# Hybrid conv and gated-delta-rule block: writing a head's 1/rms to DRAM as columns, straight from its SBUF tile

## The chip, the cores and the metric

The kernel runs on one core of one Trainium2 chip. The metric is the device time of one execution in microseconds (us). The kernel before was timed in three runs: median 1574.67 us, from 1572.23 to 1576.7.

## What is computed

Two layers work on 256 context tokens and 1024 main tokens of width 1024. A layer normalises and modulates its input, multiplies it by `w_in`, and splits the product into a convolution branch (31 taps, layer norm, gate) and four heads of a gated delta rule in both directions of time. Both branches are multiplied by `w_out` and added to the input. The part that matters here ends each head:

```
o = (o_f + flip(o_b)).transpose(0, 2, 1, 3)
zg = jax.nn.silu(z.reshape(bsz, t, DN_HEADS, DN_HEAD_DIM))
o = rms_norm(o, norm_w) * zg       # y * rsqrt(mean(y*y) + EPS) * norm_w
```

So each token of each head needs one number, 1/rms over its 128 channels, by which the head's output is multiplied.

## The kernel before, in words

All 1280 tokens lie on the free axis, in ten blocks of 128; channels lie on the 128 partitions. Layer 0 works on ten blocks, layer 1 on the eight blocks of the main tokens where the result is concerned (`xb0` = 2).

The work of a layer is cut into steps, and a string per layer in `PLAN` names their order: `K`, `Q`, `V`, `Z` are projections of a head (L376, TensorE; `Z` stores the gate to `gdr`), `A` the short convolution and the norms, `B` the inverse of a triangular matrix (its elimination runs on VectorE, L706 and L708, ends in the transposes L712 and L713, and TensorE takes it up at L729), `D` the decay rows and attention blocks, `R` the recurrence over the blocks, `N` the norm of the head's output, `C` and `T` the convolution's projections and its taps (L538, VectorE), `G` the convolution's gates, `L` its layer norm, `W` the first loads of `w_out`. The output projection (L1022) follows. `LEAD` lifts some steps' priority by a number of instructions, and `ADA_AT` says after which weight groups a slice of the modulation weights is loaded. From these priorities the order of every engine's instructions is fixed when the program is built; on the chip each engine and each DMA queue works its own list strictly in order and waits on semaphores.

Step `N` is `head_norm` (L883 on). It adds the two directions (L894, VectorE), squares (L895, ScalarE), sums over the channels with a matmul against ones, so that token sums stand as columns (L897, through L169), and loads the gate `sz` (L898, the queue of GpSimd). VectorE makes 1/rms in `st[:, 1]`, a tile of 128 partitions (tokens of a block) by ten or eight columns (blocks), with eleven small operations and three rounds of Newton's method (L899, L140 to L145). For heads 0 to 2 the columns have to become one row that lies on all partitions: TensorE turns them into ten rows of 128 (L903), ScalarE copies these out of PSUM (L905) and issues their store to a row of the DRAM tile `rdr` (L907), and GpSimd's queue reads the row back onto all partitions into `rb` (L908). `rb` is the buffer `qg[1]`, `sz` the buffer `qg[0]`, and the next head's step `D` loads its rows into the same two buffers (L665). VectorE then multiplies by the gate (L911) and by `rb` (L921), and GpSimd's queue stores the result to `ydr` (L922). Head 3 spreads its columns with matmuls instead (L918) and is not touched. There are six of these turns, three in each layer.

Of the kernel before, what the change touches and what calls it, by code (L numbers as in the profile page):

```python
# [8 lines left out]
F32 = mybir.dt.float32  # L9
# [4 lines left out]
AF = mybir.ActivationFunctionType  # L14
# [10 lines left out]
NB = T // 128  # L25
# [17 lines left out]
for _name, _w in (("nw", DEPTH * KT), ("bada", DEPTH * 24), ("cw", DEPTH * 4 * CW), ("cb", DEPTH * 4),  # L43
# [7 lines left out]


PLAN = (
# [4 lines left out]
)  # L58

ADA_AT = ((0, 2, 4, 6, 7, 8, 9, 10, 11, 12, 13, 14, 15, 16, 17, 18, 19, 20, 21, 22, 23, 24, 26, 27), (0, 3, 10, 14, 15, 16, 19, 22))


LEAD = {'O': 300, 'A': 700, 'B': 450, 'D': 1000, 'L': 1200, 'M': 0, 'N': 500, 'R': 1000, 'W': 2550}


def pos(b):
    return b * 128 + (4 if b >= 2 else 0)
# [3 lines left out]
def mixer_kernel(ctx: ExitStack, tc: tile.TileContext, xs, cst_d, wada, win, wab, gp_d, wout, fnw, out):  # L73
    nc = tc.nc
    dve, act, pool, pe = nc.vector, nc.scalar, nc.gpsimd, nc.tensor
# [6 lines left out]
    def bank(tag, bufs, shape=(128, 512)):  # L82
        return ps.tile(list(shape), F32, tag=tag, name=tag, bufs=bufs)

    def misc(shape=(128, 512)):
        return bank("pb", 2, shape)
# [4 lines left out]
    def cols(shape):  # L91
        return bank("pa", 1, shape)
# [8 lines left out]
    ident = cp.tile([128, 128], F32, name="ident")  # L101
# [35 lines left out]
    def rsqrt_small(y, x, t):  # L137

        yi = y.bitcast(I32)
        dve.tensor_scalar(out=yi, in0=x.bitcast(I32), scalar1=1, scalar2=None, op0=ALU.logical_shift_right)  # L140
        dve.tensor_scalar(out=yi, in0=yi, scalar1=-1, scalar2=0x5F3759DF, op0=MUL, op1=ADD)
        for _ in range(3):
            dve.tensor_tensor(out=t, in0=y, in1=y, op=MUL)
            dve.scalar_tensor_tensor(out=t, in0=t, scalar=-0.5, in1=x, op0=MUL, op1=MUL)
            dve.scalar_tensor_tensor(out=y, in0=t, scalar=1.5, in1=y, op0=ADD, op1=MUL)  # L145
# [21 lines left out]
    def colsum(o, w, i, start=True, stop=True):  # L167

        pe.matmul(o[:, i:i + 128], lhsT=w, rhs=ones, start=start, stop=stop)  # L169
# [3 lines left out]
    def ada_load(l, g):  # L173
        w = wp.tile([128, KT, 128], F32, tag="wst", name="wst", bufs=3)
        nc.sync.dma_start(w, wada[l, g])
        return l, g, w
# [154 lines left out]
    def later(n, f, *a):  # L331
        for _ in range(n):
            yield 1
        f(*a)
# [9 lines left out]
    def load_w(l, g, invh):  # L344
# [6 lines left out]
        if nxt_ < len(GORDER) and GORDER[nxt_][0] == l:  # L351
            prefetch(GORDER[nxt_])
            active.append(later(0, split, GORDER[nxt_]))
        if (nxt_ - 1) % (len(GORDER) // DEPTH) in ADA_AT[l]:
            held.append(ada_load(*ADA[l].pop(0)))
# [42 lines left out]
    for l in range(DEPTH):  # L398
        last = l == DEPTH - 1
        segs = XSEGS if last else SEGS  # L400
        xb0 = 2 if last else 0
        lay = ExitStack()
        hd = lay.enter_context(tc.tile_pool(name=f"hd{l}", bufs=1, side="right"))
# [479 lines left out]
        def head_norm(h, kq, ob, qg, zsc):  # L883


            t_ = qg[0].rearrange("p a b -> p (a b)")
            rb = qg[1].rearrange("p a b -> p (a b)")

            sz = t_ if h < HEADS - 1 else hd.tile([128, T], F32, tag="tmp", name="sz", bufs=4)
            pss = cols((128, NB + 127))  # L890
            st = hd.tile([128, 3, NB], F32, tag="ost", name="ost", bufs=1)
            for t0, n, v_ in segs:
                o = kq[:, 1, pos(t0 // 128):pos(t0 // 128) + n]
                dve.tensor_tensor(out=o, in0=o, in1=ob.rearrange("p a b -> p (a b)")[:, t0:t0 + n], op=ADD)  # L894
                act.activation(t_[:, t0:t0 + n], o, AF.Square)  # L895
                for b in range(t0 // 128, (t0 + n) // 128):
                    colsum(pss, t_[:, b * 128:(b + 1) * 128], b)  # L897
            nc.gpsimd.dma_start(sz[:, segs[0][0]:], gdr[l][4 + h][:, segs[0][0]:])  # L898
            dve.tensor_scalar(out=st[:, 0, xb0:], in0=pss[:, xb0:NB], scalar1=1.0 / 128, scalar2=EPS, op0=MUL, op1=ADD)  # L899
            rsqrt_small(st[:, 1, xb0:], st[:, 0, xb0:], st[:, 2, xb0:])  # L900
            if h < HEADS - 1:
                pr = cols((NB, 128))
                pe.transpose(pr[0:NB - xb0, :], st[:, 1, xb0:], ident)  # L903
                ro = hd.tile([4 * NB, 128], F32, tag="rt", name="ro", bufs=1)
                act.activation(ro[0:NB - xb0, :], pr[0:NB - xb0, :], AF.Copy)  # L905
                dr = rdr[l][16 + h:17 + h, xb0 * 128:]
                nc.scalar.dma_start(dr.rearrange("r (b t) -> (r b) t", t=128), ro[0:NB - xb0, :])  # L907
                nc.gpsimd.dma_start(rb[:, xb0 * 128:], dr.partition_broadcast(128))  # L908
            for t0, n, v_ in segs:
                o = kq[:, 1, pos(t0 // 128):pos(t0 // 128) + n]  # L910
                dve.scalar_tensor_tensor(out=o, in0=o, scalar=zsc[:, v_:v_ + 1], in1=sz[:, t0:t0 + n], op0=MUL, op1=MUL)  # L911
                if h < HEADS - 1:
                    src = rb[:, t0:t0 + n]
                else:
                    src = misc()[:, 0:n]
                    for j in range(n // 128):
                        b = t0 // 128 + j
                        pe.matmul(src[:, j * 128:(j + 1) * 128], lhsT=st[:, 1, b:b + 1].to_broadcast([128, 128]),  # L918
                                  rhs=ident, start=True, stop=True)
                if h < HEADS - 1:  # L920
                    dve.tensor_tensor(out=o, in0=o, in1=src, op=MUL)  # L921
                    nc.gpsimd.dma_start(ydr[l][4 + h][:, t0:t0 + n], o)  # L922
                else:
                    dve.tensor_tensor(out=olast[0][:, t0:t0 + n], in0=o, in1=src, op=MUL)
# [4 lines left out]
        def emit(step):  # L929
            k, i = step[0], int(step[1:] or 0)  # L930
            if k in "KQV":
                head_proj(i, "KQV".index(k))
            elif k == "A":
                with after("elim"):
                    prep[i] = head_a(i)
            elif k == "B":
                inv[i] = head_b1(i, prep[i][0], prep[i][2])
            elif k == "D":
                b2[i] = head_b2(i, *prep[i])
            elif k == "R":  # L940
                head_rec(i, prep[i][0], prep[i][2], inv[i], *b2[i])
            elif k == "N":
                head_norm(i, prep[i][0], b2[i][2][:, 1], b2[i][3], zs[i])
            elif k == "Z":
                zs[i] = head_z(i)
            elif k == "C":
                us[i] = conv_proj(i)
            elif k == "T":
                with after("elim"):
                    conv_taps(i // 3, i % 3)  # L950
            elif k == "G":
                conv_gate(i)
            elif k == "W":
                early_wout()
            elif k == "L":
                conv_norm(i)

        for step in PLAN[l].split():
            with tc.high_priority(LEAD[step[0]]) if step[0] in LEAD else nullcontext():
                emit(step)  # L960
# [10 lines left out]
        with tc.tile_pool(name=f"op{l}", bufs=1, side="right", reuse_waits="tile") as op:  # L971
# [20 lines left out]
            def out_tile(tt, tag):  # L992
                i = (tt - xb0) % 2
                y = place(f"y{i}", 896).rearrange("p (k t) -> p k t", t=128)
                yh, yl = (place(f"{t_}{i}", DM, F32R).rearrange("p (k t) -> p k t", t=128) for t_ in ("yh", "yl"))
                return tt, y, yh, yl, [bank(tag, 2) for _ in range(2)]
# [58 lines left out]

            with tc.high_priority(LEAD["O"]):
                two = [out_tile(xb0, "pj"), out_tile(xb0 + 1, "rc")]
# [33 lines left out]
            for tt in range(xb0 + 2, NB):  # L1091
                t = out_tile(tt, "pj")
# [73 lines left out]
```

## Time and profile before

| | |
|---|---|
| median of three runs | 1574.67 us |
| the profiled execution | 1572.46 us, of which the span is 1570.8 us |
| TensorE (PE) | busy 1457.3 us, 93% of the span |
| VectorE (DVE) | busy 1253.7 us, 80% |
| ScalarE (ACT) | busy 896.0 us, 57% |
| GpSimd (POOL) | busy 145.1 us, 9% |
| mean granted TensorE clock | 0.976 |

A share of busy time is a mean over stages that have different limits, so what a change is worth has to be read from the stretch in which it stands. A time in brackets behind an instruction is how long its engine sat idle before it, and the name after the arrow is what ended that wait.

### The profile page before, as it was taken

How to read it: one execution, taken by the hardware profiler on the slowest of the kernel's cores; microseconds unless marked ns; L12 is line 12 of the kernel's file. 1: busy time of each engine (PE TensorE's matmuls, PEld its weight loads, DVE VectorE, ACT ScalarE, POOL GpSimd, SP SyncE). 2: the span in 40 equal slices, each digit the busy share in tenths (PEclk: the TensorE clock that was granted, in tenths of full speed). 3: DMA queues.
4: the chain of work that ended last, by engine and by line, in shares of the span. 5: the costliest groups of instructions: out<-in, count | busy, mean ns of one | idle time of the engine just before them, and what ended most of it. 6: DMA issues, size and time to landing. Idle time of an engine off the chain costs nothing. (4 is left out here: it accounts for less than half of the span.)

```text
span 1570.8 us, 27515 instructions
## 1 busy us (share of the span) xinstructions
PE 1457.3 (93%) x10536; PEld 991.6 (63%) x10536; DVE 1253.7 (80%) x2759; ACT 896.0 (57%) x2013; POOL 145.1 (9%) x252
## 2 busy tenths in 40 slices
PE   7899899899998999899899999999899799999997
PEld 1656577577655776676787754476467476467686
DVE  3865989899679999856676556999999989987675
ACT  3757467565347764645454337576676577576321
POOL 0002010100011101101000002010110100121000
PEclk9799999999999999999999999999999999999999
DMA  9213111311143213333743113121311312253651
GB/s 299 113 55 109 45 62 54 138 45 55 58 135 108 76 54 106 112 135 124 250 156 104 55 41 110 39 75 44 112 62 41 121 54 69 82 175 120 213 171 54
DMA packets 83328, 158.21 MB, mean 101 GB/s; under 512 B 5670, under 2 KB 52764, under 8 KB 83196
## 3 DMA queue, kind: packets, MB, share of 16 engines
q1 hardware_dynamic: 67408, 96.74, 19.8%
q0 software_dynamic: 15280, 59.52, 10.3%
q8 instruction: 83, 1.36, 0.3%
q14 instruction: 49, 0.40, 0.1%
q10 hardware_dynamic: 508, 0.19, 0.0%
HBM read 125.43 MB, written 30.99 MB: 100 GB/s over the span
## 5 line engine op out<-in xcount | busy, mean ns | idle before, releaser
L376 PE MATMUL pj<-hhi,whi 128*128 128x512 f16 (+1 forms) x1184 | 424.8, 359 | 4.2 <-ACT raw L596 3.9
L376 PE MATMUL pj<-hhi,wlo 128*128 128x512 f16 (+1 forms) x1184 | 424.4, 359 | 1.2 <-DVE wlo L300 1.1
L376 PE MATMUL pj<-hlo,whi 128*128 128x512 f16 (+1 forms) x1184 | 425.2, 359 | 0.0
L376 PEld LDWEIGHTS <-whi 128*128 128x128 f16 x2368 | 231.5, 99 | 179.3 <-issue 20.2
L538 DVE SCALAR_TENSOR_TENSOR acc<-u,cws,acc 128x960 f32<-128x960 f32 (+26 forms) x240 | 231.0, 963 | 1.2
L376 PEld LDWEIGHTS <-wlo 128*128 128x128 f16 x1184 | 117.4, 99 | 90.5 <-issue 7.9
L1022 PE MATMUL pj<-woh,yh 128*128 128x512 f32 x256 | 102.2, 399 | 7.4 <-ACT yh L1010 7.4
L1022 PE MATMUL pj<-woh,yl 128*128 128x512 f32 x256 | 103.0, 402 | 0.7 <-DVE yl L1011 0.7
L286 ACT ACTIVATE whi<-wst 128x1024 bf16<-128x1024 f32 x56 | 59.0, 1053 | 77.3 <-PE pj L376 69.5
L1022 PE MATMUL pj<-wol,yh 128*128 128x512 f32 x256 | 102.2, 399 | 0.0
L623 DVE SCALAR_TENSOR_TENSOR kq<-raw,cst,kq 128x1284 f32<-128x1284 f32 (+1 forms) x64 | 93.5, 1477 | 7.9 <-ACT kq L621 7.7
L706 DVE TENSOR_TENSOR et<-xp 128x30 f32<-128x30 f32 (+14 forms) x240 | 82.4, 343 | 5.3
L708 DVE TENSOR_TENSOR xp<-xp,et 128x30 f32<-128x30 f32 (+14 forms) x240 | 80.5, 335 | 5.3
L859 ACT ACTIVATE vs<-rc,hs 128x128 f32<-128x128 f32 x144 | 52.1, 367 | 56.1 <-PE rc L856 55.6
L300 DVE SCALAR_TENSOR_TENSOR wlo<-wst,w_s,whi 128x1024 f16<-128x1024 f32 x56 | 73.9, 1320 | 9.4 <-ACT whi L299 9.2
L299 ACT ACTIVATE whi<-wst,w_s 128x1024 f16<-128x1024 f32 x56 | 64.2, 1146 | 26.9 <-DVE w_s L298 26.3
L164 PE MATMUL pw<-scond,wst 128*128 128x128 f32 x512 | 71.7, 277 | 0.1
L164 PEld LDWEIGHTS pw<-scond,wst 128*128 128x128 f32 x512 | 64.3, 192 | 2.3 <-DVE cst__7698 L562 0.3
L866 PE MATMUL rc<-vs,ktm 128*128 128x128 f32 x288 | 60.9, 300 | 3.8 <-ACT vn L862 2.8
L866 PEld LDWEIGHTS rc<-vs,ktm 128*128 128x128 f32 x288 | 43.4, 189 | 29.8 <-ACT vn L862 23.8
L1022 PEld LDWEIGHTS pj<-woh,yh 128*128 128x128 f32 x256 | 48.9, 191 | 19.0 <-ACT yh L1010 7.8
L623 DVE SCALAR_TENSOR_TENSOR v<-raw,cst,v 128x1284 f32<-128x1284 f32 x32 | 50.0, 1561 | 13.5 <-ACT v L621 13.3
(367 smaller groups left out, 2958.7 us busy)
## 6 DMA issues: line engine op xcount, KB each, us to landing
wst<-in_win_dram SPq DMA_DIRECT2D x56, 512.0 KB
row<-rdr POOLq DMA_DIRECT2D x35, 640.0 KB, 4.5
wst<-in_wada_dram SPq DMA_DIRECT2D x32, 512.0 KB
x<-in_xs_dram SPq DMA_DIRECT2D x20, 512.0 KB
ast<-in_wada_dram SPq DMA_DIRECT2D x8, 1024.0 KB
wst<-in_wout_dram SPq DMA_DIRECT2D x16, 512.0 KB
y<-ydr SPq DMA_DIRECT2D x14, 448.0 KB
a<-cdr SPq DMA_DIRECT2D x9, 512.0 KB
```

Source lines behind the costliest of these rows:

```text
L164: pe.matmul(o, lhsT=w[:, k, :], rhs=scond[:, k:k + 1, :].to_broadcast([128, 64, 2]), start=(k == 0), stop=(k == KT - 1))
L286: act.activation(hi.bitcast(BF16), st, AF.Square, accum_out=ss)
L299: act.activation(hi, st, AF.Identity, scale=s[:, 0:1])
L300: dve.scalar_tensor_tensor(out=lo, in0=st, scalar=s[:, 0:1], in1=hi, op0=MUL, op1=SUB)
L376: pe.matmul(pj[:, 0:n], lhsT=a[:, k, :], rhs=b[:, k, t0:t0 + n], start=(i == 0), stop=(i == 3 * KT - 1))
L538: gates["big"] = dve.scalar_tensor_tensor(out=ao, in0=ui, scalar=cws[:, 0, j:j + 1], in1=ao, op0=MUL, op1=ADD)
L623: gates["big"] = dve.scalar_tensor_tensor(out=dst, in0=src[:, o0 + j:o0 + j + n], scalar=col("sw", j0 + j), in1=dst, op0=MUL, op1=ADD)
L706: dve.tensor_tensor(out=ev, in0=xp[:, j + 1:, j:j + 1].to_broadcast([128, ni, j]), in1=xp[:, j:j + 1, 0:j].to_broadcast([128, ni, j]), op=MUL)
L708: dve.tensor_tensor(out=xp[:, j + 1:, 0:j], in0=xp[:, j + 1:, 0:j], in1=ev, op=ADD)
L859: act.activation(vss[d], pns[d], AF.Identity, scale=hs[:, 2 + d, bs[d]:bs[d] + 1])
L866: pe.matmul(pkv, lhsT=ktm[:, bs[d], :], rhs=vss[d], start=True, stop=True)
L1022: pe.matmul(pj[hf], lhsT=a[:, k, :], rhs=w[k][:, hf * 512:(hf + 1) * 512], start=k == KORDER[0] and i == 0, stop=k == KORDER[-1] and i == 2)
```

## The change

The three instructions of the turn (L903, L905, L907) go. The store to DRAM is issued on GpSimd's queue straight from `st`: token t of block b goes to address 128 b + t of the row, so neighbouring elements of a partition land 512 bytes apart, and each element of four bytes is a piece of its own. The read back stays. In the same edit three steps of the plan of layer 0 and some of layer 1 change places, one index of `ADA_AT` moves, and three entries of `LEAD` change.

```diff
 PLAN = (
-    "Q0 K0 V0 C0 A0 K1 Q1 V1 B0 Z0 A1 D0 T0 T1 Q2 B1 R0 N0 C1 T2 D1 K2 C2 T3 V2 T4 T5 A2 R1 Z1 V3 B2 Q3 K3 C3 T6 Z3 "
-     "D2 N1 A3 T7 T8 B3 Z2 G0 T9 G2 T10 G1 R2 N2 D3 R3 T11 L0 L1 W L2 L3 N3 L4 G3",
+    "Q0 K0 V0 C0 A0 K1 Q1 V1 B0 Z0 A1 T0 T1 D0 Q2 B1 R0 N0 C1 T2 D1 K2 C2 T3 V2 T4 T5 A2 R1 Z1 V3 B2 Q3 K3 C3 T6 Z3 "
+     "D2 N1 A3 T7 T8 B3 Z2 G0 T9 G2 T10 G1 R2 D3 N2 R3 T11 L0 L1 W L2 L3 N3 L4 G3",
...
-     "A3 T7 Z3 Z2 T8 D2 B3 T9 T10 G2 G1 G0 R2 T11 D3 L0 L1 L2 L3 L4 R3 W N2 G3 N3",
+     "A3 T7 Z3 Z2 T8 D2 B3 T9 G2 G0 G1 T10 R2 T11 D3 L0 L1 N2 L2 L3 L4 R3 W G3 N3",
 )
-ADA_AT = ((0, 2, 4, 6, ...
+ADA_AT = ((0, 2, 5, 6, ...
-LEAD = {'O': 300, 'A': 700, 'B': 450, 'D': 1000, 'L': 1200, 'M': 0, 'N': 500, 'R': 1000, 'W': 2550}
+LEAD = {'O': 300, 'A': 750, 'B': 450, 'D': 1000, 'L': 900, 'M': 0, 'N': 500, 'R': 1000, 'W': 2650}
...
             if h < HEADS - 1:
-                pr = cols((NB, 128))
-                pe.transpose(pr[0:NB - xb0, :], st[:, 1, xb0:], ident)
-                ro = hd.tile([4 * NB, 128], F32, tag="rt", name="ro", bufs=1)
-                act.activation(ro[0:NB - xb0, :], pr[0:NB - xb0, :], AF.Copy)
                 dr = rdr[l][16 + h:17 + h, xb0 * 128:]
-                nc.scalar.dma_start(dr.rearrange("r (b t) -> (r b) t", t=128), ro[0:NB - xb0, :])
+                nc.gpsimd.dma_start(dr.rearrange("r (b t) -> t (r b)", t=128), st[:, 1, xb0:])
                 nc.gpsimd.dma_start(rb[:, xb0 * 128:], dr.partition_broadcast(128))
```

## Rows read from the trace of the kernel before

**Rows 1.** Page, part 1: engine, busy us (share of span), instructions.

```profile
PE 1457.3 (93%) x10536; PEld 991.6 (63%) x10536; DVE 1253.7 (80%) x2759; ACT 896.0 (57%) x2013; POOL 145.1 (9%) x252
```

**Rows 2.** Waits of TensorE: waiter, what ended it, total us, times, longest us.

```profile
PE pb L729 <- DVE xtr L713: 17.0, 6, 4.2
PE pa L903 <- DVE ost L145: 9.8, 5, 3.1
...
PE pa L903 <- DVE w_s L298: 0.5, 1, 0.5
```

**Rows 3.** Timeline of TensorE, layer 0, head 1: start us, duration us, instruction, [idle before].

```profile
472.72 0.27 PE L903 MATMUL pa<-ident,ost 128*10 128x128 f32 x1 [3.12 <-DVE ost L145]
472.83 0.38 PE L376 MATMUL pj<-hlo,whi 128*128 128x512 f16 x1
...
490.19 0.82 PE L729 MATMUL pb<-xtr,tt 32*32 32x32 f32 x40 [3.49 <-DVE md L181]
```

**Rows 4.** Busy us of PE, PEld, DVE, ACT, POOL by stretch; clock, DMA share, GB/s.

```profile
280.00:320.00 40.00, 33.51 (x286) 19.44 (x286) 36.12 (x77) 20.91 (x48) 7.12 (x12) 0.91 0.36 132
...
308.00:312.00 4.00, 3.18 (x45) 1.88 (x46) 3.70 (x4) 3.98 (x10) 0.71 (x2) 0.50 0.01 4
...
400.00:440.00 40.00, 39.89 (x231) 22.72 (x230) 24.88 (x42) 13.80 (x20) 2.13 (x4) 1.00 0.29 90
...
468.00:472.00 4.00, 1.60 (x8) 0.51 (x6) 4.00 (x18) 0.00 (x0) 0.00 (x0) 1.00 0.44 133
...
1080.00:1120.00 40.00, 37.53 (x232) 23.85 (x231) 37.19 (x86) 19.95 (x48) 7.64 (x9) 1.00 0.41 137
...
1400.00:1440.00 40.00, 39.97 (x257) 30.70 (x255) 28.23 (x82) 25.26 (x61) 2.38 (x4) 1.00 0.36 120
```

**Rows 5.** Waits of ScalarE, as in Rows 2.

```profile
ACT ro L905 <- PE pa L903: 21.0, 5, 6.9
```

**Rows 6.** Timeline of GpSimd's queue, layer 0, head 1: the read back of the row.

```profile
475.05 0.53 POOL L908 DMA_DIRECT2D row<-rdr  x1 [0.98 <-DMA rdr<-ro]
```

**Rows 7.** Timeline of VectorE: last Newton step and first L921, four steps N.

```profile
283.50 0.16 DVE L145 SCALAR_TENSOR_TENSOR ost<-ost 128x10 f32<-128x10 f32 x1
...
292.40 0.42 DVE L921 TENSOR_TENSOR kq<-kq,row 128x256 f32<-128x256 f32 x1
...
472.41 0.16 DVE L145 SCALAR_TENSOR_TENSOR ost<-ost 128x10 f32<-128x10 f32 x1
...
480.54 0.42 DVE L921 TENSOR_TENSOR kq<-kq,row 128x256 f32<-128x256 f32 x1
...
1101.66 0.16 DVE L145 SCALAR_TENSOR_TENSOR ost<-ost 128x8 f32<-128x8 f32 x1
...
1109.77 1.35 DVE L921 TENSOR_TENSOR kq<-kq,row 128x512 f32<-128x512 f32 x1 [0.37 <-DMA row<-rdr]
...
1226.57 0.16 DVE L145 SCALAR_TENSOR_TENSOR ost<-ost 128x8 f32<-128x8 f32 x1
...
1234.37 0.69 DVE L921 TENSOR_TENSOR kq<-kq,row 128x512 f32<-128x512 f32 x1
```

**Rows 8.** DMA issues: out<-in, queue, count, KB each, median us from issue to landing.

```profile
ydr<-a POOLq DMA_DIRECT2D x9, 512.0 KB, 3.4
...
xres<-x POOLq DMA_DIRECT2D x8, 512.0 KB, 2.9
...
ydr<-kq POOLq DMA_DIRECT2D x3, 128.0 KB, 2.0
```

**Rows 9.** The read back (L908) by itself.

```profile
DMA to landing us min/median/max: 3.6/4.8/5.4
```

**Rows 10.** Page, part 3: hardware queue of SyncE, packets, MB, share of 16 engines.

```profile
q1 hardware_dynamic: 67408, 96.74, 19.8%
```

**Rows 11.** Issue of a store in 512 pieces, and of a load in 128, on GpSimd.

```profile
1440.31 0.76 POOL L579 DMA_DIRECT2D ydr<-a  x1 [1.60 <-DVE cst__14743 L140]
1441.38 0.55 POOL L898 DMA_DIRECT2D sz<-gdr  x1 [0.31 <-DMA ydr<-a]
```

**Rows 12.** Page, part 2, last line: packets of the whole run by size.

```profile
DMA packets 83328, 158.21 MB, mean 101 GB/s; under 512 B 5670, under 2 KB 52764, under 8 KB 83196
```

More of the change, by code (lines that the diff above doesn't have):

```diff
@@ L53 @@
 PLAN = (
[2 rows of a table removed]
[2 rows of a table added]
     "V0 K0 Q0 A0 C0 K1 Q1 V1 Z0 B0 T0 C1 A1 D0 T1 T2 R0 N0 B1 Q2 D1 K2 V2 Z1 T3 A2 C2 T4 R1 K3 B2 Q3 T5 V3 T6 C3 N1 "
[1 row of a table removed]
[1 row of a table added]
 )
-ADA_AT = ((0, 2, 4, 6, 7, 8, 9, 10, 11, 12, 13, 14, 15, 16, 17, 18, 19, 20, 21, 22, 23, 24, 26, 27), (0, 3, 10, 14, 15, 16, 19, 22))
-LEAD = {'O': 300, 'A': 700, 'B': 450, 'D': 1000, 'L': 1200, 'M': 0, 'N': 500, 'R': 1000, 'W': 2550}
+ADA_AT = ((0, 2, 5, 6, 7, 8, 9, 10, 11, 12, 13, 14, 15, 16, 17, 18, 19, 20, 21, 22, 23, 24, 26, 27), (0, 3, 10, 14, 15, 16, 19, 22))
+LEAD = {'O': 300, 'A': 750, 'B': 450, 'D': 1000, 'L': 900, 'M': 0, 'N': 500, 'R': 1000, 'W': 2650}
 def pos(b):
```

## The prediction

> **What bounds the kernel now.** The page's busy shares come first [rows 1]: TensorE 93%, VectorE 80%. One mean hides two regimes, so the second view is the busy time by stretch [rows 4]. At 400 to 440 us and at 1400 to 1440 us TensorE is full (39.89 and 39.97 of 40 us) and VectorE has over 11 us to spare: there TensorE sets the pace. At 280 to 320 us and 1080 to 1120 us VectorE is busy 36 to 37 us, which with the short gaps between hundreds of small operations is about all it can do, and TensorE sits idle 2.5 to 6.5 us: there VectorE sets the pace. The steps N that the change touches stand in this second kind of stretch, beside the elimination of the next head's step B.
>
> The third view is TensorE's list of waits [rows 2]. It waits at the turn L903 for the last Newton step in all 9.8 + 0.5 = 10.3 us over six times, and 17.0 us over six times at L729, where it takes up the elimination's result. The fourth is the timeline around one N [rows 3]: the turn stood in the middle of a projection, TensorE held the next matmul of that projection for 3.12 us behind a turn of ten columns, and went on 0.11 us after the turn's start. 17 us later it waited again, 3.49 us, at L729. This pair, a wait at L903 and then one at L729, is what the reader should see: the first stall can be removed and come back as the second.
>
> **The turn removed.** TensorE: 10.3 us of waits and six slots of 0.11 us [rows 3], 11.0 us. ScalarE: six copies and six issues, about 0.5 us each, and 21.0 us in which its list stood at L905 [rows 5]; it is 57% busy, and I count this at nothing, since the evictions and weight splits behind it fed the projection that stood still too. If VectorE came to wait for those splits, ScalarE's relief would be worth something; nothing is lost there. VectorE executes the same operations as before.
>
> How much of the 11.0 us stays? The bounds are 0 and 11.0. Zero, if every microsecond won comes back at the following L729, because elimination and Newton steps are VectorE's own work and no faster. All, if the orders remade by the edit hold enough other work for TensorE there. The rows of VectorE-bound stretches [rows 4] are nearer the lower end, those of the full-TensorE stretches that follow each L729 the upper: an engine that sets the pace later profits if it enters that stretch ahead. I take half: -5.5 us.
>
> **The new store.** It takes the turn's place in the path from the last Newton step to L921. Today that path has two parts: until L908 is issued, 475.05 - 472.57 = 2.5 us [rows 6, 7], and 4.8 us to landing [rows 9]. VectorE reaches L921 8.74, 7.97, 7.95 and 7.64 us after the last Newton step in heads 0 and 1 of the two layers [rows 7], in the third case after a wait of 0.37 us already; for head 2 the gate arrives much later than the row, so its two turns have cover. With a store that lands s after its issue, and an estimated 0.2 us for two hand-overs, the row is there s + 5.0 us after the last Newton step. L921 then waits s + 5.0 less those four allowances: in all 4s - 12.3 us when all four are short.
>
> The trace has no store in pieces of four bytes, so s is bounded. From below: a store of 128 KB in 128 pieces lands in 2.0 us; a store of 512 KB in 512 pieces takes 3.4 us against 2.9 us for as many bytes in 128 pieces [rows 8], 1.3 ns for each further piece. With 1280 pieces that is 2.0 + 1152 x 0.0013 = 3.5 us. From above: SyncE's queue spent 0.198 x 16 x 1570.8 us / 67408 = 74 ns of an engine on a packet, of 1.4 KB on average [rows 10]; 1280 / 16 = 80 such in a row are 5.9 us, with the 2.0 us 7.9 us. I take 3.5 us, since it comes from the same queue and direction. The waits are then 0, 0.5, 0.6 and 0.9: +2.0 us. At 7.9 us they are 4.2, 4.9, 5.0 and 5.3: +19.3 us. Behind L921 on VectorE stands the rest of the elimination, so such a wait moves L713 and with it TensorE's L729 by as much.
>
> The Trainium skill speaks against this store: "DMA: Bandwidth & Descriptors", section "Rules for kernel authors", says that a transfer whose last dimension is not contiguous becomes one descriptor per element and should be rearranged. Its section "Bandwidth" gives about 10.5 ns a packet; by that, as an estimate, 1280 would need 13.4 us on top of the fixed part, and the sum would be some 50 us higher. The trace's 1.3 ns a piece does not agree, but it was read from larger pieces.
>
> **GpSimd's queue.** A store in 512 pieces took 0.76 us to issue, a load in 128 pieces 0.55 us [rows 11]; by the same slope the new issue is 1.2 us, six times 7 us on an engine that is 9% busy [rows 1]. The queue then stands at L908 until the store has landed, as it does now [rows 6]. Behind it wait the next head's second row load (L665) and the write of the elimination's diagonal (L709); L665 cannot start before L921 anyway. Nothing for this beyond s, with L709 as the one that suffers next.
>
> **Plan, ADA_AT, LEAD.** No engine's work changes, only orders. A move of D or N against its neighbours shifts which projection stands before an L729; the mean wait there is 17.0 / 6 = 2.8 us [rows 2]. With three such moves the bounds are -8.5 and +8.5 us. One has a sign in the rows: in layer 1 the taps T10 go behind three gates, out of VectorE's full stretch toward 1400 us, where VectorE has 11.8 us to spare [rows 4]. I take half a wait, -1.4 us.
>
> **Sum.** -5.5 + 2.0 - 1.4 = -4.9 us. The profiled execution took 1572.46 us, giving 1567.6; the median lies 2.2 us above that execution, so 1569.8 us on its scale.
>
> **Rivals.**
> - *The stall only moves (no change).* Every wait saved at L903 is added to the one at L729, with +2.0 us for L921 and nothing or little from the plan: 1573 to 1577 us. For it: the pair of waits in rows 3; against it: the stretches after L729 are TensorE's.
> - *The element store is late (slower).* At L921 VectorE waits 4s - 12.3 us; the gains of 6.9 us are used up at s = 4.8 us. At the middle of the bounds, 5.7 us, the waits are 10.5 us: 1574.7 - 6.9 + 10.5 = 1578 us, or 1585 us if the stall only moves too. For it: allowances of 8 us that already hold one wait; against it: the order is remade, and L921 can be put later.
> - *The gathered wait lowers the clock (slower).* TensorE waited 3.12 us before the turn at full granted clock [rows 3, 4], but behind the wait for the elimination, at 308 to 312 us, the granted clock was 0.50, the lower level of 1.2 GHz [rows 4]. If the two waits become one, the fall can be longer in the four steps concerned: 4 us at half clock lose 2 us each, +8 us with nothing kept, 1583 us.
> - *The store is not cut into elements.* Then s is about 2.0 us, no wait is added, and the sum is 1567.8 us; it counts with the forecast.
>
> **How the numbers follow.** About 0.3%, 4.7 us, is what a measurement can tell from no change. The forecast, a gain over that, has 0.42; its own range is 1561 (all 11.0 us kept, a wait of 2.8 us gained by the plan) to 1570. The stall that only moves has 0.30. The late store has 0.20 and the clock, or a plan that orders worse, 0.08: slower 0.28. The range for eight in ten goes from 1558 to 1585 us, from the full gain with some of the plan's bound to the late store with nothing kept.
>
> **What would show it.** No L903, L905, L907; TensorE's waits for `ost` gone but for head 3; the sum at L729 between 17 and 27 us, near 22 if half is kept. About 6900 more packets under 512 B than the 5670 of now [rows 12], if elements go one by one (3 x 1280 + 3 x 1024). The store's landing near 3.5 us, its issue near 1.2 us, and waits of VectorE at L921 for the row of 2 us in all. It is wrong if the landing is over 4.8 us with L921 waiting for it, if L729 has taken up the whole 10 us, or if a wait outside steps N and B moved by more than 5 us: then the plan decided.

## The result, and the profile after

The changed kernel takes 1617.44 us (median of four runs, 1616.16 to 1620.12), the kernel before 1575.68 us beside it: a ratio of 1.0263 [1.0241, 1.0284], 42 us slower. The forecast was 1569.8 us with 1585 as its upper end: wrong in sign and in size. In this kernel the store is L903, the read back L904, the gate multiply L907, the row multiply L917, the store to `ydr` L918 and the output projection L1018.

Start with the page's busy times (part 1) and its last line on packets, to be held against [rows 1, 12].

```profile
PE 1466.5 (91%) x10530; PEld 991.9 (61%) x10530; DVE 1248.4 (77%) x2759; ACT 893.7 (55%) x2007; POOL 151.0 (9%) x258
...
DMA packets 83460, 158.21 MB, mean 98 GB/s; under 512 B 5856, under 2 KB 52896, under 8 KB 83328
```

VectorE, which works through the same operations, is busy as long as before in a span of 1615.6 us against 1570.8: the time was lost waiting. Which wait, its list says (what waited, for what, total us, times, longest us).

```profile
DVE kq L917 <- DMA row<-rdr: 40.1, 4, 11.7
```

Before, the same wait came once, with 0.37 us [rows 7]. TensorE's list, against [rows 2]:

```profile
PE pb L729 <- DVE xtr L713: 23.5, 6, 9.9
PE pw L292 <- DVE md L181: 18.8, 5, 10.9
PE pj L376 <- ACT raw L596: 18.3, 4, 7.1
...
PE pj L376 <- DVE u L509: 8.0, 2, 7.3
```

L903's 10.3 us are gone, but these four come to 68.6 us, where the kernel before has 23.1. They are other engines' standstills seen from TensorE: VectorE's and, behind `ACT raw L596`, ScalarE's, which in layer 0's second head waited for GpSimd's L670 and so for a late row load of the next head:

```profile
495.19 3.03 ACT L818 ACTIVATE na<-na,hs 128x128 f32<-128x128 f32 x10 [10.66 <-POOL na L670]
```

Next, the store, the read back, the next head's row loads (L665) and the weight loads (L320), each by its line: instructions with the time of their issue (min/median/max ns), and the us from issue to landing.

```profile
L903 POOL DMA_DIRECT2D rdr<-ost x6: 912/940/972, 282.6 to 1375.5; - x6
...
DMA to landing us min/median/max: 9.6/9.8/10.1
...
L904 POOL DMA_DIRECT2D row<-rdr x6: 531/540/557, 292.5 to 1386.2; - x6
...
DMA to landing us min/median/max: 4.8/6.3/9.1
...
L665 POOL DMA_DIRECT2D row<-rdr x32: 528/539/680, 130.5 to 1426.8; - x32
...
DMA to landing us min/median/max: 4.1/5.3/13.2
...
L320 SPq DMA_DIRECT2D wst<-in_win_dram x56: 327/328/3054, 37.5 to 1408.4; - x56
...
DMA to landing us min/median/max: 3.4/3.6/12.2
```

The store of 5 KB lands after 9.8 us, where one of 128 KB took 2.0 [rows 8]. The read back is slower too (6.3 against 4.8 us [rows 9]), and so are single row and weight loads. The timelines of GpSimd's queue and VectorE around the first N of layer 0 put these in order:

```profile
282.58 0.97 POOL L903 DMA_DIRECT2D rdr<-ost  x1 [4.29 <-DVE ost L145]
283.91 0.55 POOL L665 DMA_DIRECT2D row<-rdr  x1 [0.36 <-DVE kq L907]
292.52 0.54 POOL L904 DMA_DIRECT2D row<-rdr  x1 [8.06 <-DMA rdr<-ost]
...
301.62 1.63 DVE L917 TENSOR_TENSOR kq<-kq,row 128x256 f32<-128x256 f32 x3 [11.74 <-DMA row<-rdr]
```

In the third head of a layer, whose gate comes later, L917 has cover; there GpSimd's queue pays: its list has 18.2 us before L904 that end in an issue (two waits, the longer 9.7 us), with the gate's stores queued behind; what that costs is read at `token_perm` below. What the DMA engines do meanwhile is in the same first N by single microseconds (us of the stretch; busy us of TensorE, weight load, VectorE, ScalarE, GpSimd; then granted clock, DMA share, GB/s).

```profile
284.00:285.00 1.00, 1.00 (x12) 0.90 (x10) 0.96 (x4) 0.37 (x1) 0.46 (x1) 1.00 0.55 5
285.00:286.00 1.00, 1.00 (x12) 0.95 (x10) 1.00 (x6) 0.58 (x1) 0.00 (x0) 1.00 0.02 0
...
287.00:288.00 1.00, 0.73 (x8) 0.44 (x7) 1.00 (x2) 0.00 (x0) 0.00 (x0) 1.00 0.00 0
288.00:289.00 1.00, 0.58 (x4) 0.30 (x5) 0.97 (x4) 0.00 (x0) 0.00 (x0) 1.00 0.32 51
289.00:290.00 1.00, 1.00 (x11) 1.00 (x11) 0.81 (x3) 0.00 (x0) 0.00 (x0) 1.00 0.12 20
...
292.00:293.00 1.00, 1.00 (x10) 0.83 (x9) 0.00 (x0) 0.00 (x0) 0.47 (x1) 1.00 0.10 15
293.00:294.00 1.00, 1.00 (x6) 0.49 (x5) 0.00 (x0) 0.00 (x0) 0.06 (x1) 1.00 0.94 92
...
295.00:296.00 1.00, 1.00 (x6) 0.47 (x5) 0.00 (x0) 0.00 (x0) 0.00 (x0) 1.00 0.90 348
```

This is the view to learn from. From 284 to 285 us the engines move 5 GB/s for one microsecond: 5 KB, the store's 1280 pieces entire, at 0.55 x 16 us / 1280 = 6.9 ns of an engine on each. As the trace records them, the pieces are through in a microsecond. Then the engines move 0 to 51 GB/s for eight, though L665's load was issued at 283.91 and SyncE's weight loads at 287.91 and 288.33, until the store lands and everything moves at once.

### The profile page after: what moved, and what is told of

Same layout as the page of the kernel before. It is cut to its first block, busy times and chain, and to the rows that moved or that the text cites. A ratio compares the mean times of both kernels' runs of the same rounds, so it can differ in the third digit from the quotient of the medians.

```text
span 1615.6 us, 27493 instructions
## 1 busy us (share of the span) xinstructions
PE 1466.5 (91%) x10530; PEld 991.9 (61%) x10530; DVE 1248.4 (77%) x2759; ACT 893.7 (55%) x2007; POOL 151.0 (9%) x258
## 5 line engine op out<-in xcount | busy, mean ns | idle before, releaser
L376 PE MATMUL pj<-hhi,whi 128*128 128x512 f16 (+1 forms) x1184 | 428.5, 362 | 27.5 <-ACT raw L596 18.3
L376 PE MATMUL pj<-hlo,whi 128*128 128x512 f16 (+1 forms) x1184 | 428.5, 362 | 0.0
L376 PE MATMUL pj<-hhi,wlo 128*128 128x512 f16 (+1 forms) x1184 | 427.5, 362 | 0.7 <-DVE wlo L300 0.6
L376 PEld LDWEIGHTS <-whi 128*128 128x128 f16 x2368 | 232.6, 100 | 209.3 <-issue 51.2
L376 PEld LDWEIGHTS <-wlo 128*128 128x128 f16 x1184 | 118.4, 100 | 95.8 <-issue 12.8
L1018 PE MATMUL pj<-woh,yh 128*128 128x512 f32 x256 | 101.6, 397 | 6.5 <-ACT yh L1006 6.5
L1018 PE MATMUL pj<-woh,yl 128*128 128x512 f32 x256 | 101.9, 398 | 0.7 <-DVE yl L1007 0.7
L1018 PE MATMUL pj<-wol,yh 128*128 128x512 f32 x256 | 101.5, 396 | 0.0
L300 DVE SCALAR_TENSOR_TENSOR wlo<-wst,w_s,whi 128x1024 f16<-128x1024 f32 x56 | 72.7, 1297 | 10.7 <-ACT whi L299 10.2
L818 ACT ACTIVATE na<-na,hs 128x128 f32<-128x128 f32 x144 | 44.0, 388 | 44.3 <-POOL na L670 44.3
L596 ACT ACTIVATE raw<-pj,wm 128x512 f32<-128x512 f32 (+1 forms) x68 | 42.0, 618 | 37.2 <-PE pj L376 34.9
```

Source lines behind the costliest of these rows:

```text
L300: dve.scalar_tensor_tensor(out=lo, in0=st, scalar=s[:, 0:1], in1=hi, op0=MUL, op1=SUB)
L376: pe.matmul(pj[:, 0:n], lhsT=a[:, k, :], rhs=b[:, k, t0:t0 + n], start=(i == 0), stop=(i == 3 * KT - 1))
L1018: pe.matmul(pj[hf], lhsT=a[:, k, :], rhs=w[k][:, hf * 512:(hf + 1) * 512], start=k == KORDER[0] and i == 0, stop=k == KORDER[-1] and i == 2)
```

## The experiments

The first theory was the rival of the prediction: the store is late, and its landing is all of the loss. Its rivals were the remade plan, and a store that also holds up other transfers. Where an expectation names a theory by a letter, its sentence says what that theory states. Sizes are ratios to the kernel before on the same chip, in 95% intervals where there are several runs.

**The plan or the store.** `plan_only` is the kernel before with the new `PLAN`, `ADA_AT` and `LEAD`; `store_only` is the changed kernel with the old ones.

```diff
-PLAN, ADA_AT, LEAD of the kernel before
+PLAN, ADA_AT, LEAD of the changed kernel
```

> The turn and the row store of before, with the plan, ADA_AT and LEAD of after. Theory L (the landing of the element store, 9.6 to 10.1 us, is what VectorE and GpSimd's queue wait out): the loss is not here, 1570 to 1582 us. Rival P (the new order of steps is what costs): most of the 42 us is here, 1600 us or more.

> The element store of after, with the plan, ADA_AT and LEAD of before. Theory L: the whole loss is here, 1610 to 1625 us, with some 40 us of waits of VectorE for the row. Rival P: 1570 to 1590 us.

Measured: 1572.8 us, 0.9988 [0.9967, 1.0009], and 1625.84 us, 1.0331 [1.0289, 1.0372]; its store lands in 10.7 us and L917 waits 43.5 us. The loss is the store's; the plan can't be told from no change.

**Is it only the wait?** `no_wait` reads back an older row, so that nothing waits for the store; `no_wait_act` also issues the store on ScalarE's queue, `act_queue` does that alone, with the wait.

```diff
-                nc.gpsimd.dma_start(rb[:, xb0 * 128:], dr.partition_broadcast(128))
+                nc.gpsimd.dma_start(rb[:, xb0 * 128:], rdr[l][4 * h:4 * h + 1, xb0 * 128:].partition_broadcast(128))
...
-                nc.gpsimd.dma_start(dr.rearrange("r (b t) -> t (r b)", t=128), st[:, 1, xb0:])
+                nc.scalar.dma_start(dr.rearrange("r (b t) -> t (r b)", t=128), st[:, 1, xb0:])
```

> As after, but the read back takes a row of rdr that was stored long before, so that the element store runs and nothing waits for it; the output heads 0 to 2 are scaled by the wrong row. Theory L: the waits for the row go and the time falls to 1565 to 1580 us, below before if the 11 us of TensorE's turns are partly kept. Rival C (the 6912 small writes slow other transfers or GpSimd): stays over 1595 us.

> As after, but the element store is issued on ScalarE's hardware queue in place of GpSimd's. The run without the wait showed that row loads issued behind the element store on GpSimd's queue landed only after 11 us. Theory F (the store itself takes some 10 us and holds what is queued behind it, on GpSimd's queue): the read back still waits for the store, 8 to 10 us after the last Newton step, but the row loads (L665) land in 4 to 6 us again; 1590 to 1612 us. Rival G (GpSimd is slow at writing the descriptors, the elements are quick): the store lands in 2 to 4 us and the time is 1570 to 1582 us.

> As the run without the wait (the read back takes an old row, so the output is scaled by the wrong row), but with the element store on ScalarE's queue, so that neither a wait nor GpSimd's queue stands behind it. Theory F: 1565 to 1582 us, as the plan alone with the turn gone. Rival C (the small writes slow other transfers on the engines they share): over 1590 us.

Measured: 1636.47 us, 1.0387 [1.0341, 1.0432]; 1622.72 us, 1.0297 [1.0272, 1.0323]; 1633.33 us, 1.0361 [1.0338, 1.0384]. L917 waits no longer in the first and the last, and nothing is won. In `no_wait` the row loads by their line (first fence), GpSimd's wait for them and two of TensorE's waits (second) show where it went:

```profile
L665 POOL DMA_DIRECT2D row<-rdr x32: 528/539/680, 130.6 to 1443.7; - x32
...
DMA to landing us min/median/max: 4.1/5.4/14.9
```

```profile
POOL na L670 <- DMA row<-rdr: 62.7, 11, 12.2
...
PE pb L729 <- DVE xtr L713: 31.5, 5, 12.5
PE pb L729 <- DVE md L181: 21.6, 2, 11.1
```

"Only the wait" fell: a row load behind the store lands up to 14.9 us after its issue (8.1 at most in the kernel before), and what it feeds waits in L917's place. ScalarE's queue is no way out. The store lands there in 11.6 us, and in `no_wait_act` loads on GpSimd's queue, another queue than the store's, take up to 15.2 us. So the store holds transfers whose issuer has nothing to do with it. The Trainium skill, "DMA: Bandwidth & Descriptors", section "Rules for kernel authors", says that spreading transfers over the issuing engines doesn't help bandwidth, as all run on the same 16 DMA engines; these runs agree that another queue doesn't help. On ScalarE's queue the elements appear as packets, 12624 under 512 B, and on GpSimd's they don't: that is why the changed kernel shows only 5856.

**Number of pieces, place, neighbours.** `half_pieces` stores 640 (512) elements, `one_column` 128 in one stretch of 512 bytes; the other blocks are scaled by what lies there. `own_tile` stores to a DRAM tile of its own that nobody reads; `spread` gives each partition 512 bytes of its own there and takes every second word.

```diff
+                nc.gpsimd.dma_start(dr[:, 0:hb * 128].rearrange("r (b t) -> t (r b)", t=128), st[:, 1, xb0:xb0 + hb])
...
+                nc.gpsimd.dma_start(dr[:, 0:128].rearrange("r (b t) -> t (r b)", t=128), st[:, 1, xb0:xb0 + 1])
...
+                dr = odr[l][h:h + 1, xb0 * 128:]
...
+                dr = sdr[l][h].rearrange("t (b two) -> t b two", two=2)[:, 0:NB - xb0, 0]
```

> As after, but only the first half of the columns is stored by elements and read back (640 or 512 elements; the second half of the tokens is scaled by what the buffer held). If the landing grows with the number of elements, it falls from 9.6 to 10.1 us to 5 to 6.5 us and the time to 1580 to 1600 us; if it does not depend on their number, it stays at 9 us or more.

> As after, but only one column is stored by elements and read back: 128 elements of four bytes, all in one stretch of 512 bytes (the other tokens are scaled by what the buffer held). Half the elements landed no sooner (9.5 to 11.8 us), so the number of elements is not what counts. Theory N (neighbours: 128 elements from all engines written into the same 512 bytes are taken one after the other): still 8 us or more. Theory E (a price per element that half the elements happened to hide): 2 to 3 us, as other stores of 128 pieces.

> As the run without the wait, but the elements go to a DRAM tile of their own that nothing reads (output scaled by the wrong row). If the late row loads come from reading near the rows being written, in the same DRAM tile, they land in 4 to 6 us again and the time falls to 1570 to 1585 us. If the store holds up every transfer wherever it goes, row loads of up to 13 us remain and the time is 1625 us or more.

> As the run with a tile of its own and without the wait, with as many elements of four bytes, but each partition writes into its own 512 bytes, every second word, so that no two partitions share such a stretch (output scaled by the wrong row). Theory N: it lands in 2 to 4 us, no row load is late, 1568 to 1585 us. Theory E: it lands in 9 us or more, 1625 us or more.

Measured: 1631.11, 1619.26 and 1636.2 us (one run each) and 1623.74 us, 1.0317 [1.0283, 1.0351]. The landings have medians of 10.3, 8.4, 11.0 and 8.3 us. A tenth of the pieces lands hardly sooner, and a row that nobody reads is no quicker. In `spread`, elements 512 bytes from the next partition's land a little sooner than in `own_tile`, which also reads back an older row (8.3 against 11.0 us), and a row load still takes up to 16.8 us. So neither number nor place nor neighbours is the main cause.

**Larger pieces.** `token_major` writes a partition's ten (eight) numbers side by side, 128 pieces of 40 (32) bytes, and VectorE reads the row with a stride. `dve_turn` turns 32 by 32 blocks on VectorE and stores pieces of 128 bytes in four transfers, `dve_turn_act` does so on ScalarE's queue. `two_columns` and `four_columns` store two or four of the columns, 128 pieces of 8 or 16 bytes.

```diff
+                nc.gpsimd.dma_start(dr.rearrange("r (t b) -> t (r b)", b=nb), st[:, 1, xb0:])
...
+                dve.transpose(out=tr, in_=s32)
+                for q in range(4):
+                    nc.gpsimd.dma_start(dq[q], tr[32 * q:32 * q + nb, :])
...
+                nc.gpsimd.dma_start(dr[:, 0:256].rearrange("r (t b) -> t (r b)", b=2), st[:, 1, xb0:xb0 + 2])
```

> As after, but each partition's ten or eight numbers go to DRAM side by side, one piece of 40 or 32 bytes per partition, and the multiply reads the row with a stride. Theory L with the cost in the number of pieces: 128 pieces land in about 2 us, as the 128-piece stores of before, the waits go, 1565 to 1578 us. Theory L with the cost in writes that are smaller than 512 bytes, whatever their number: landing stays near 9 us and the time near 1615 us. A strided read of VectorE at half rate would add 0.7 us to each of 15 multiplies, about 10 us.

> As after, but VectorE turns the columns in 32x32 blocks (one small operation) and four stores of ten or eight pieces of 128 bytes go out on GpSimd's queue; the multiply reads the row in order. Theory F: landings of about 2 us each, no 5 us for strided multiplies as in the run with 40 byte pieces, 1570 to 1577 us. If the turn gone from TensorE is worth its 10 us, 1565 us; if that stall only moves to the next wait on VectorE, 1572 us or more.

> As the run that turns on VectorE in 32x32 blocks, but its four stores are issued on ScalarE's queue. If that run's 1583 us came from the 24 issues of 0.5 us on GpSimd's queue, 1570 to 1577 us; if it came from TensorE's stall moving on to its next wait on VectorE, 1578 to 1588 us.

> Only the first two columns of 1/rms are stored, token by token: 128 pieces of 8 bytes (a partition's two neighbouring elements); the row's other blocks are scaled by what lies in the buffer (left out). If only pieces of 4 bytes are slow, the store lands in 2 to 3 us like the pieces of 40 bytes, VectorE's wait for the row falls under 5 us in all and the time is near 1580 us. If smallness as such is slow (a price that falls as pieces grow), it lands in 6 to 8 us, the wait stays over 20 us and the time over 1605 us.

> As before with four columns: 128 pieces of 16 bytes; the other blocks are scaled by what lies in the buffer (left out). If only 4 bytes are slow: landing 2 to 3 us, near 1580 us, as with 8 bytes. If the price falls with size: landing 3 to 6 us, between the 8.4 us of 4 bytes and the 1.9 us of 40 bytes, and the time between 1580 and 1605 us.

> The same kernel as two_columns (128 pieces of 8 bytes; the row's other blocks are scaled by what lies in the buffer, left out), since TensorE ran at less than half its usual pace through all of that execution, while VectorE's busy time was as ever. If that was the execution and not the kernel, the time is near 1580 us now. If only pieces of 4 bytes are slow, the store lands in 2 to 3.5 us and VectorE's wait for the row stays under 15 us in all; if smallness as such is slow, it lands in 6 to 8 us with waits over 20 us and a time over 1605 us.

Measured: 1580.3 us, 1.0022 [1.0002, 1.0041]; 1583.11 us, 1.0034 [1.0013, 1.0055]; 1593.43 us, 1.0117 [1.0082, 1.0153], above both of its expectations, for a reason that isn't shown; for `four_columns` 1577.83 us in one run. The first run of `two_columns` took 3640.47 us, with a 128x512 matmul at 759 ns on average instead of 362 and VectorE busy 1259.9 us as ever; what slowed TensorE there isn't known. Repeated, it took 1602.68 us, 1.0182 [1.0102, 1.0261]. The DMA issues of `one_column`, `two_columns_again`, `four_columns` and `token_major`, each with 128 pieces (count, KB each, median us to landing), make a ladder of 4, 8, 16 and 40 (32) bytes:

```profile
rdr<-ost POOLq DMA_DIRECT2D x6, 0.5 KB, 8.4
```

```profile
rdr<-ost POOLq DMA_DIRECT2D x6, 1.0 KB, 3.9
```

```profile
rdr<-ost POOLq DMA_DIRECT2D x6, 2.0 KB, 2.6
```

```profile
rdr<-ost POOLq DMA_DIRECT2D x3, 5.0 KB, 1.7
rdr<-ost POOLq DMA_DIRECT2D x3, 4.0 KB, 2.1
```

More bytes land sooner: 6.5 us above the 1.9 us of the largest at 4 bytes, 2.0 at 8, 0.7 at 16. L917's waits for the row fall with it: 32.4 us at 4 bytes, 16.8 at 8, 10.1 at 16. The 8-byte landing lies between the two that were expected; 16 bytes alone would also fit "only 4 bytes are slow". The landings can be compared, the times of these kernels only roughly: nearly every edit makes the program's builder sort the engines' lists anew. `one_column` and `two_columns_again` have the same lists; 1619 us (one run) against 1603 comes from the pieces, and from a read back of one block or of two. `two_columns_again` and `four_columns`, 25 us apart, differ in order as well.

**The same order, other pieces.** `token_perm` settles this. It is the changed kernel with the store's pieces alone altered, and every engine's list is the same, instruction by instruction.

```diff
-                nc.gpsimd.dma_start(dr.rearrange("r (b t) -> t (r b)", t=128), st[:, 1, xb0:])
+                nc.gpsimd.dma_start(dr.rearrange("r (t b) -> t (r b)", b=NB - xb0), st[:, 1, xb0:])
```

> The changed kernel with one difference: the store writes a partition's ten (or eight) numbers side by side, 128 pieces of 40 (32) bytes, and the row is read back and used as if it lay in the order of the changed kernel, so that each token is scaled with another token's number (left out: the right one). Every engine's list of instructions is the same as the changed kernel's, one by one, which holds for none of the runs before. If the four-byte pieces cost the 42 us, the store lands near 2 us, VectorE's wait for the row (40.1 us) falls under 3 us, no row load lands later than 8 us, and the time is 1570 to 1582 us. If the order that came out of the edit costs them, the landing falls as well but the time stays over 1605 us. In between, the two share it in that proportion. What remains against the kernel before (1575 us) is the worth of the turn's removal with this order: below 1570 us would mean that the 11 us of TensorE were a gain after all.

Measured: 1575.94 us over 12 runs, 1.0002 [0.9990, 1.0015]. In four fences: its page; L903, L665 and L917 by their lines (under L917 what its engine waited for, us, times); TensorE's waits; and the first of the microseconds shown above.

```profile
PE 1467.8 (93%) x10530; PEld 993.0 (63%) x10530; DVE 1252.7 (79%) x2759; ACT 894.0 (57%) x2007; POOL 146.2 (9%) x258
```

```profile
L903 POOL DMA_DIRECT2D rdr<-ost x6: 538/544/548, 281.6 to 1346.3; - x6
...
DMA to landing us min/median/max: 1.7/2.0/3.6
...
L665 POOL DMA_DIRECT2D row<-rdr x32: 528/539/680, 128.3 to 1387.1; - x32
...
DMA to landing us min/median/max: 4.1/5.0/7.4
...
L917 DVE TENSOR_TENSOR kq<-kq,row x15: 417/684/1004, 289.8 to 1386.1; 128x512 f32<-128x512 f32 x12, 128x256 f32<-128x256 f32 x3
...
  DMA row<-rdr: 1.7, 2
```

```profile
PE pb L729 <- DVE xtr L713: 14.5, 6, 4.1
PE pw L292 <- DVE md L181: 11.5, 6, 3.0
```

```profile
284.00:285.00 1.00, 1.00 (x11) 0.98 (x10) 1.00 (x6) 0.59 (x1) 0.09 (x1) 1.00 0.65 195
285.00:286.00 1.00, 1.00 (x11) 1.00 (x11) 1.00 (x4) 0.92 (x2) 0.00 (x0) 1.00 1.03 374
286.00:287.00 1.00, 0.49 (x5) 0.20 (x5) 1.00 (x2) 0.00 (x0) 0.00 (x0) 1.00 0.99 410
```

L665's load, issued behind this store too, runs at 195 to 410 GB/s where it crept before. With one order, the spans differ by 1615.6 - 1576.7 = 38.9 us, and the size of the pieces makes it. The waits at L917 differ by 40.1 - 1.7 = 38.4 us, but it is partly chance that the two agree. Held against each other instruction by instruction, TensorE's two lists drift apart by 9 to 10 us in three of the four steps N that wait at L917 and by 6 in the other, some 35 us; by some 8 us more in the third head of layer 1, where L917 has cover; and some 4 us are made good in between. Those 8 us pass through GpSimd's queue: the gate's store is issued behind L904, ScalarE (L602) waits for that store, and VectorE and TensorE wait behind ScalarE. The same two waits in the changed kernel and in `token_perm`:

```profile
1393.37 0.69 ACT L602 ACTIVATE sgz<-pj,wm 128x512 f32<-128x512 f32 x1 [10.59 <-DMA gdr<-sgz]
1397.47 0.19 PE L292 MATMUL pw<-wss,onesb 128*128 128x1 bf16 x1 [10.85 <-DVE md L181]
```

```profile
1356.16 0.69 ACT L602 ACTIVATE sgz<-pj,wm 128x512 f32<-128x512 f32 x1 [2.65 <-DMA gdr<-sgz]
1360.26 0.18 PE L292 MATMUL pw<-wss,onesb 128*128 128x1 bf16 x1 [2.92 <-DVE md L181]
```

And with a quick store the change is worth nothing.

**Is there a form that wins?** `strided_sums` lets the column sums take every tenth (eighth) token, so that the quick store lays the row down in order and nothing is read with a stride on VectorE; `strided_sums_bp` is that with the old plan.

```diff
+                tv = t_[:, xb0 * 128:].rearrange("p (t b) -> p b t", b=NB - xb0)
+                for b in range(NB - xb0):
+                    colsum(pss, tv[:, b, :], xb0 + b)
```

> Nothing left out. The column sums of heads 0 to 2 take every tenth (eighth) token instead of 128 neighbours, so that partition t of the ten columns holds ten neighbouring tokens; the store then writes pieces of 40 (32) bytes straight in the order of the row, and VectorE's multiply reads the row without a stride (token_major paid 5.4 us there). Price: the ten sums can't start before the last square, about 1 us a step, and TensorE's weights are read with a stride. The order is sorted anew. If the turn's removal is worth nothing (token_perm), 1572 to 1580 us; if the strided multiply hid a gain, below 1570 us.

> The same with the plan, the load points and the leads of the kernel before. The plan alone measured 0.9988 [0.9967, 1.0009], so this is expected within 4 us of strided_sums; more than that, either way, would be the price of an order.

Measured: 1580.43 us, 1.0028 [1.0009, 1.0048], and 1583.07 us, 1.0041 [1.0026, 1.0057]. No form beats the kernel before. The stride seems only to have changed its payer; the column sums of `strided_sums` (duration ns min/median/max):

```profile
L169 PEld LDWEIGHTS pa<-ones,row x144: 186/322/336, 273.1 to 1456.9; 128*128 128x128 f32 x144
L169 PE MATMUL pa<-ones,row x144: 272/390/504, 273.2 to 1457.0; 128*128 128x128 f32 x144
```

In the changed kernel the medians are 192 and 275 ns. Of the 144, heads 0 to 2 issue 108; 108 x 0.115 us are an estimated 12 us more of TensorE. In `token_major` VectorE paid: L920 took 1086 ns against 685, 5.4 us in all.

## Why the prediction was wrong

**The price of the store** is the step that failed. Both ends of s, 3.5 and 7.9 us, were too low: 9.8 us were measured. The lower end carried 1.3 ns a piece over from pieces of 1 KB and more [rows 8], the upper 74 ns a packet from SyncE's queue [rows 10]. Both make the price grow with the number of pieces. The runs show one that hardly depends on the number (8.4 us for 128, 9.8 for 1024 or 1280) and falls with their size. No row of the kernel before had a piece of that size, and rows of larger ones could not bound it.

The formula for L921's waits, 4s - 12.3, gives 26.9 us at s = 9.8; 40.1 were measured. The four read backs took 27.4 us from issue to L917 instead of 4 x 4.8, 8.2 more; the loads held back now ran beside them. By the timelines VectorE reached L917 in all 29.9 us after the last Newton steps instead of 32.3 (of which 0.4 was a wait already), and the hand-overs, put at 0.2 us a step without a row, took about 0.8, in all 2.6 us more. So 26.9 + 8.2 + 2.4 + 2.6 = 40.1.

**GpSimd's queue**, priced at "nothing for this beyond s", failed too. The prediction gave the third heads cover because their gate comes late. But the gate's stores stand behind L904 on this queue, and in layer 1 that cost TensorE some 8 of the 38.9 us. And the next head's first row load, issued right behind the store, landed after up to 13.2 us instead of 8.1 at most before, which ScalarE and TensorE then waited for.

**The late store** was the right rival, with a chance of 0.20, and its deciding point of 4.8 us was well passed. Its price of 1578 to 1585 us was too low: it rested on the middle of the bounds for s, and took the store to delay its own row alone. That it holds transfers on all queues stood in no step.

**The sentence on the Trainium skill**, "DMA: Bandwidth & Descriptors", section "Bandwidth", had the sum some 50 us higher, and the measured time is 48 us above the forecast. That nearness is luck: by 10.5 ns a packet, 128 elements cost an estimated 1.3 us on top of the fixed part; 8.4 us to landing were measured. The engines spend 6.9 ns on an element, and the time passes after that. The rule of its section "Rules for kernel authors", to rearrange so that the last dimension is contiguous, was the one to follow here.

**The turn removed**, -5.5 us, failed as well. In `token_perm` no late store covers it: L903's waits are gone and the time is the same. Against `plan_only`, which has the same plan and keeps the turn, the difference is 1.0002 - 0.9988, +2.2 us, with an uncertainty of some 3.9 us (the two intervals added in squares), which leaves out -5.5. The page and TensorE's waits of `plan_only` show where the gain went:

```profile
PE 1461.8 (93%) x10536; PEld 989.8 (63%) x10536; DVE 1252.7 (80%) x2759; ACT 895.8 (57%) x2013; POOL 142.9 (9%) x252
...
PE pb L729 <- DVE xtr L713: 11.5, 6, 3.8
...
PE pa L903 <- DVE ost L145: 9.1, 5, 3.0
...
PE pw L292 <- DVE md L181: 3.3, 3, 2.2
```

From there to `token_perm` the 9.1 us at L903 go, while L729 gains 3.0 us and L292 8.2. TensorE stands idle 1571.1 - 1461.8 = 109.3 us in `plan_only` and 1576.7 - 1467.8 = 108.9 us in `token_perm`. So by these two executions nothing of the 11.0 us stayed, and taking half was the mistake. (Of the 10.3 us at L903 the list puts 0.5 down to another operation of VectorE, L298 [rows 2].) "The stall only moves", at 0.30, was right for this part, though it went to L292 more than to the one place it named. L292 also waits for a result of VectorE, behind the work that VectorE has there anyway. The third rival, a lower clock, isn't shown: over all runs beside each other the mean granted clock has medians of 0.971 (12 runs of `token_perm`) and 0.974 (17 of the kernel before), and no run separates that from scatter.

**The plan**, -1.4 us: 0.9988 [0.9967, 1.0009] is -1.9 us and can't be told from nothing.

**The signs.** L729's 23.5 us lay in the foretold 17 to 27 us and so hid that L292 and L376 had become as large. Some 6900 more small packets were foretold and 186 came, as GpSimd's queue doesn't show elements as packets: that sign would have said "not cut" of a store that was. The issue took 0.94 us against 1.2. The sign that spoke was the landing, with L917's wait behind it.

## What to carry to other kernels

A store that scatters single four-byte elements can hold up the loads of every queue seen here for some ten microseconds, so put the turn elsewhere: on TensorE with rows to store, or in how columns are laid out, with pieces of 32 bytes or more. Before pricing a transfer by a neighbour's row, see whether that row has pieces of the same size, and keep an open upper end if none has. And where an edit makes the builder sort the program anew, look for the one edit that leaves every list alone: only such a pair shows what the edit itself costs, and by which waits.

## What was not expected of the hardware

A store in four-byte pieces lands 6 to 13 us after its issue in these runs (layer medians 8.3 to 13.2), for 128 or 1280 pieces, from either queue, to any of the places tried. In the first N its pieces pass the DMA engines within one microsecond, as the trace records them, and loads on its own and on SyncE's queue then move 0 to 51 GB/s until it has landed, where behind a store in larger pieces they move 195 to 410. The price falls with the piece: 8.4, 3.9, 2.6 and 1.9 us at 4, 8, 16 and 32 to 40 bytes. What happens in that time isn't shown. The Trainium skill, "Collectives: The Full Stack", section "Rules for kernel authors", has buffers aligned to 32 bytes to avoid a read-modify-write by the hardware. These runs don't show such a rule of alignment at work: of the 40-byte pieces at most every fourth can start at a multiple of 32 bytes, and they land in 1.7 us, the 32-byte pieces in 2.1.
